# Second feed-forward projection's token operands split into high and low parts in the first projection's stage

## The chip, the cores and the metric

The kernel runs on one core of a Trainium2 chip. The time is the device time of one launch in microseconds (us), and less is better. The kernel before took 1708.27 us, the median of three runs (1705.85 to 1709.84).

## What is computed

One decoder layer for a prompt of 1024 tokens and a group of 8 x 8 sample tokens, 1088 tokens in all: a normalised, conditioned input, three mixers (attention, short convolution, pooling), an output projection, and a gated feed-forward block. The change touches only the feed-forward block:

```python
def swiglu(h, w_up, w_down):
    a, b = jnp.split(h @ w_up, 2, axis=-1)
    return (jax.nn.silu(a) * b) @ w_down
    ...
    x = x + gate1 * (jnp.concatenate([o_attn, y_conv, y_pool], axis=-1) @ w_out)
    h = rms_norm(x, norm2) * (1 + scale2) + shift2
    x = x + gate2 * swiglu(h, w_up, w_down)
```

The model width is 1024, the hidden width 2816, which is 22 tiles of 128. Everything is float32.

## The kernel before, in words

**Layout and products.** Features lie on the 128 partitions, tokens along the free dimension in four quarters of 272. Both projections use a Strassen-Winograd scheme: a 2 x 2 block product by seven products. In the first projection the two token blocks are two quarters (pair p = 0: quarters 0 and 1, p = 1: quarters 2 and 3). Each float32 operand of a product is written as a high part, rounded to the matmul's float32r format, and a low part, the rest; a product is then three matmuls (high x high, high x low, low x high). `split` (L163) makes the two parts: one ACT activation for the high part and one subtraction on DVE, or on POOL, for the low part.

**First projection** (`ffn`, L1623, and `up`, L1533). It goes over 22 hidden tiles j. For each j there is a unit for p = 0 and one for p = 1, of seven products with twelve matmuls each. DVE and ACT combine the banks to the gated hidden block `f_g`, which POOL finishes (L1581). Beside it the weights of the next j are summed (`w_s`, mostly POOL) and split (`w_hi` on ACT, `w_lo` on DVE).

**Between the two** (`down_operands`, L1586). The seven token operands that the second projection wants of a pair of hidden tiles (k = j // 2, eleven of them) and a p are three blocks as they are and four differences `f_T`, made on POOL. `store` sends each to the DRAM tensor `g_d` in float32; the list `forming` spreads the differences over the steps of the following p = 0 unit, one per product.

**Second projection** (`down_run`, L1793). It goes over six groups e of hidden tile pairs: two pairs in each of the first five groups, one in the last (`DOWN`, L30). A group is four passes (h = output half, p) of seven products and two output tiles: 28 x 2 slots, 336 matmuls in a full group, 168 in the last. `down_tokens` (L1715) loads each operand (`g_raw`) and splits it (`g_hi` on ACT, `g_lo` on DVE or POOL). `down_weights` (L1680) loads, sums (`w_s`, POOL) and splits the weights (`w_lo` or `d_lo`, DVE) of each half. After a product the bank goes to the residual x2: either straight by DVE (`down_gate`, L1745, which reads the bank) or by ACT into `d_m` (L1755) and from there by a POOL addition `x<-x,d_m`. Which weight or token step stands in which slot is a list of due slots (`down_plan`, L1760). x2 itself is loaded from `x1_d` at the start of this stage (`x1_load`, L1804).

The program is recorded in this order and then reordered per engine by a scheduler. All loads and stores named here go through SP's one queue, in its order.

Of the kernel before, what the change touches and what calls it, by code (L numbers as in the profile page):

```python
# [29 lines left out]
DOWN = (2, 2, 2, 2, 2, 1)  # L30
# [30 lines left out]
class Kernel:  # L61
# [1471 lines left out]
    def up(self, fp, j, p, W, H, step):  # L1533
# [4 lines left out]
        for y, x in enumerate(PRODUCTS):  # L1538
# [47 lines left out]
    def down_operands(self, pool, j, p, g, r):  # L1586
# [3 lines left out]
        end = j == NH - 1 and p  # L1590

        def store(dst, src):
            if end:
                nc.gpsimd.dma_start(dst, src)
            else:
                self.stores.append((self.steps + 2, dst, src))

        if j % 2:
            store(self.g_d[:, p, 1:3, j // 2], g)
        else:  # L1600
            store(self.g_d[:, p, 0, j // 2], g[:, 0])
# [5 lines left out]
        def form(x, a, b):  # L1607
            T[x] = pool.tile([P, HALF], F32, name="f_T", bufs=4)
            self.combine(T[x], a, T[b] if isinstance(b, int) else b, OP.subtract, HALF, r, "pool")
            store(self.g_d[:, p, STORED[x], j // 2], T[x])  # L1610

        self.forming += [lambda v=v: form(*v) for v in ((5, B1[:, 1], B1[:, 0]), (6, B2[:, 1], 5), (4, B2[:, 0], 6),
                                                        (7, B2[:, 1], B1[:, 1]))]
        if end:
# [8 lines left out]
    def ffn(self, wp, fp, H, state, ahead):  # L1623
# [21 lines left out]
        for n, (j, ps) in enumerate(runs):  # L1645
# [3 lines left out]
            for z, p in enumerate(ps):  # L1649
# [4 lines left out]
                def step(y, z=z, last=last, m=len(ps)):  # L1654
# [3 lines left out]
                    if self.forming and (not last or j == NH - 1):  # L1658
                        self.forming.pop(0)()
# [55 lines left out]
    def down_tokens(self, pool, steps, out):  # L1715

        nc = self.nc
        raw = []

        def load():  # L1720
            if todo:
                k0, q, e, p, x = todo.pop(0)
                t = pool.tile([P, 2, HALF], F32, name="g_raw", bufs=4)
                nc.sync.dma_start(t[:, :q], self.g_d[:, p, STORED[x], k0:k0 + q])
                raw.append((t, self.use("dma", 0.38 * q, self.t["pe"]) + 2.0))

        todo = list(steps)
        for _ in range(3):
            load()
        yield  # L1730
        for k0, q, e, p, x in steps:
            load()
            t, at = raw.pop(0)
            hi = pool.tile([P, 2, HALF], F32R, name="g_hi", bufs=15)
            lo = pool.tile([P, 2, HALF], F32R, name="g_lo", bufs=15)
            f = lambda a: a[:, :q].rearrange("p k t -> p (k t)")
            self.split(f(hi), f(lo), f(t), q * HALF, at, None)
            out[e, p, x] = (hi, lo)
# [21 lines left out]
    def down_plan(self):  # L1760

        k0, groups = 0, []
        for q in DOWN:
            groups.append((k0, q))
            k0 += q
        W, G, plan = {}, {}, []
        tok = [(k0, q, e, p, x) for e, (k0, q) in enumerate(groups) for p in range(2) for x in DOWN_PRODUCTS]
        self.d_tok = None
        for e, (k0, q) in enumerate(groups):
# [406 lines left out]
```

## Time and profile before

| | us |
|---|---|
| median of three runs | 1708.27 |
| the profiled execution | 1706.47 |
| its span, first to last instruction | 1704.6 |
| first projection's units, roughly | 930 to 1437 |
| second projection's matmuls, roughly | 1437 to 1697 |
| TensorE busy over the span | 1609.1 (94%) |
| DVE, ACT, POOL busy | 1113.6, 817.8, 706.9 |

Times within the run are microseconds from the start of the span. A busy matmul row overlaps its neighbours, so lost matmul time is read here from the number of matmuls in a stretch, not from the busy share.

### The profile page before, as it was taken

How to read it: one execution, taken by the hardware profiler on the slowest of the kernel's cores; microseconds unless marked ns; L12 is line 12 of the kernel's file. 1: busy time of each engine (PE TensorE's matmuls, PEld its weight loads, DVE VectorE, ACT ScalarE, POOL GpSimd, SP SyncE). 2: the span in 40 equal slices, each digit the busy share in tenths (PEclk: the TensorE clock that was granted, in tenths of full speed). 3: DMA queues.
4: the chain of work that ended last, by engine and by line, in shares of the span. 5: the costliest groups of instructions: out<-in, count | busy, mean ns of one | idle time of the engine just before them, and what ended most of it. 6: DMA issues, size and time to landing. Idle time of an engine off the chain costs nothing. (4 is left out here: it accounts for less than half of the span.)

```text
span 1704.6 us, 34455 instructions
## 1 busy us (share of the span) xinstructions
PE 1609.1 (94%) x11961; PEld 1414.5 (83%) x11961; DVE 1113.6 (65%) x2830; ACT 817.8 (48%) x1878; POOL 706.9 (41%) x814
## 2 busy tenths in 40 slices
PE   6999999998998999999899789999999999889998
PEld 2999997887776566666699779999999998889997
DVE  4603326686665766866699986555555556988877
ACT  3512215245766776766675643332333334555554
POOL 3101110013331322222106476445555555898976
PEclk9899999998999999999999989999999999999999
DMA  9555564226654644432783223225222225744423
GB/s 341 170 179 177 162 208 143 80 63 196 196 171 125 199 138 146 143 92 83 233 244 90 92 72 117 96 97 191 97 100 96 96 97 187 240 128 132 131 82 122
DMA packets 177120, 245.08 MB, mean 144 GB/s; under 512 B 25889, under 2 KB 132578, under 8 KB 176626
## 3 DMA queue, kind: packets, MB, share of 16 engines
q1 hardware_dynamic: 157090, 215.37, 40.4%
q0 software_dynamic: 5840, 16.10, 2.9%
q10 hardware_dynamic: 14016, 11.41, 2.2%
q8 instruction: 95, 1.56, 0.4%
q14 instruction: 79, 0.65, 0.1%
HBM read 202.33 MB, written 44.67 MB: 145 GB/s over the span
## 5 line engine op out<-in xcount | busy, mean ns | idle before, releaser
L135 PE MATMUL bank<-b_hi,w_hi 128*128 128x272 f32 x1232 | 352.3, 292 | 9.2 <-DVE f_v L1551 4.5
L135 PE MATMUL bank<-b_lo,w_hi 128*128 128x272 f32 x1232 | 356.0, 291 | 2.9 <-DVE b_lo L160 2.9
L135 PE MATMUL bank<-b_hi,w_lo 128*128 128x272 f32 x1232 | 352.0, 290 | 1.3 <-DVE w_lo L160 1.3
L135 PEld LDWEIGHTS bank<-b_hi,w_hi 128*128 128x128 f32 x1232 | 232.3, 191 | 12.3 <-ACT b_hi L164 5.1
L135 PEld LDWEIGHTS bank<-b_lo,w_hi 128*128 128x128 f32 x1232 | 234.4, 190 | 4.5 <-DVE b_lo L160 4.4
L135 PEld LDWEIGHTS bank<-b_hi,w_lo 128*128 128x128 f32 x1232 | 233.1, 190 | 2.5 <-DVE w_lo L160 2.3
L160 POOL TENSOR_TENSOR w_s<-w_raw 128x512 f32<-128x512 f32 (+1 forms) x122 | 167.3, 1373 | 149.4 <-DVE w_lo L160 133.0
L1050 POOL TENSOR_SCALAR P<-P,st 128x128 f32<-128x128 f32 (+12 forms) x192 | 112.0, 592 | 259.2 <-DVE st L1048 86.3
L160 DVE TENSOR_TENSOR w_lo<-w_raw,w_hi 128x512 fp32r<-128x512 f32 (+2 forms) x129 | 115.0, 898 | 100.7 <-ACT w_hi L164 85.8
L164 ACT ACTIVATE w_hi<-w_raw 128x512 fp32r<-128x512 f32 (+2 forms) x130 | 86.4, 674 | 150.5 <-PE bank L135 100.5
L160 DVE TENSOR_TENSOR w_lo<-w_s,w_hi 128x512 fp32r<-128x512 f32 (+1 forms) x144 | 130.3, 908 | 43.1 <-ACT w_hi L164 39.2
L160 POOL TENSOR_TENSOR x<-x,d_m 128x272 f32<-128x272 f32 x144 | 140.1, 994 | 22.9 <-DVE x L1745 11.1
L135 PE MATMUL bank<-stream 128*128 128x128 f32 x1056 | 134.1, 285 | 6.8 <-DMA stream<-in_cacheA 6.7
L135 PEld LDWEIGHTS bank<-stream 128*128 128x128 f32 x1056 | 129.0, 200 | 13.8 <-issue 8.7
L164 ACT ACTIVATE w_hi<-w_s 128x512 fp32r<-128x512 f32 (+1 forms) x144 | 89.0, 624 | 102.4 <-PE bank L135 51.5
L135 PE MATMUL bank<-h_hi,w_hi 128*128 128x384 f32 (+1 forms) x384 | 130.9, 341 | 2.4 <-ACT py L865 2.3
L135 PE MATMUL bank<-h_hi,w_lo 128*128 128x384 f32 (+1 forms) x384 | 127.1, 331 | 0.0
L1042 ACT ACTIVATE P<-P,st 128x128 f32<-128x128 f32 (+12 forms) x192 | 113.2, 591 | 28.4 <-DVE st L1033 13.8
L135 PE MATMUL bank<-h_lo,w_hi 128*128 128x384 f32 (+1 forms) x384 | 126.6, 330 | 0.0
L135 PE MATMUL bank<-g_hi,w_hi 128*128 128x272 f32 x308 | 91.8, 300 | 14.5 <-DVE x L1745 8.2
L139 PEld LDWEIGHTS bank<-ident,P 128*128 128x128 f32 (+1 forms) x592 | 63.2, 138 | 50.7 <-issue 33.6
L1033 DVE CUSTOM_DVE_ANT_0 P<-bank,m_slc 128x256 f32<-128x256 f32 (+5 forms) x136 | 68.1, 513 | 54.2 <-PE bank L135 29.2
(368 smaller groups left out, 4114.8 us busy)
## 6 DMA issues: line engine op xcount, KB each, us to landing
wada<-in_wada SPq DMA_DIRECT2D x96, 256.0 KB, 5.3
stream<-in_cacheA SPq DMA_DIRECT2D x192, 128.0 KB, 3.3
w_raw<-in_wup SPq DMA_DIRECT2D x48, 512.0 KB, 4.3
unit<-in_cacheB SPq DMA_DIRECT2D x152, 128.0 KB, 2.3
g_raw<-g_d SPq DMA_DIRECT2D x70, 272.0 KB, 3.1
stream<-in_cacheB SPq DMA_DIRECT2D x104, 128.0 KB, 2.2
w_raw<-in_wout SPq DMA_DIRECT2D x24, 512.0 KB, 4.7
g_d<-f_T SPq DMA_DIRECT2D x84, 136.0 KB, 1.8
```

The lines of the kernel that those rows point to most:

```text
L135: return self.nc.tensor.matmul(out, lhsT, rhs, start=start, stop=stop, skip_group_check=chain)
L139: self.nc.tensor.transpose(out, in_, self.ident)
L160: (self.nc.vector if eng == "dve" else self.nc.gpsimd).tensor_tensor(out, a, b, op=op)
L164: self.nc.scalar.activation(hi, src, AF.Copy)
L1033: nc.vector.tensor_tensor_reduce(out=Pt[:, h, col:col + n], in0=S[:, p0:p0 + n], in1=mk, scale=-1.0, scalar=3e38, op0=OP.add, op1=OP.min, ...
L1042: nc.scalar.activation(Ps, Ps, AF.Exp, scale=-1.0, bias=sy[:, 0:1], accum_out=sy[:, 1:2])
L1050: nc.gpsimd.tensor_scalar(Ps, Ps, sy[:, 3:4], 0.0, op0=OP.mult, op1=OP.add)
```

## The change

Lines are those of the two files; the changed file's are some 6 to 15 higher at the same place.

- The seven operands of a pair of hidden tiles and a p are split in the first projection's stage, by `split` with `eng=None`, into a new tile `f_s` (three buffers, in a pool `gs` on the left side), and stored to `g_d` as high and low part side by side. The differences are made two to a tile, so a set is stored by four DMAs in place of six. Each set has eight steps in `forming`, which now advances in every unit: seven steps in a p = 0 unit, three (products 0, 3 and 6) in a p = 1 unit.
- Three of the 22 sets stay as they were (k = 0 with p = 0, and k = 10 with both p): they go unsplit to a DRAM tensor `g_r` and are split in the second projection.
- `DOWN` becomes (1,2), (3,4), (5,6), (7,8), (9), (0,10): the group with one pair is now the fifth, and the last holds pairs 0 and 10.
- Tokens of the first five groups are loaded with both parts by one DMA straight into the operand tile `g` (14 buffers); only the last group's are split there.
- The operands of p = 0 of the first projection (`b_hi`, `b_lo`) are one tile per product and part, as large as a `g` tile, where they were one per i with all seven products in it; `g` tiles later lie where they were.
- The second pass' tokens of the first group are issued after the first x2 loads, and the second half's weights of that group are due later.

```diff
-DOWN = (2, 2, 2, 2, 2, 1)
+DOWN = ((1, 2), (3, 4), (5, 6), (7, 8), (9,), (0, 10))
+RAW = (0, 10)
...
+            if i == 0:
+                self.first = [[pool.tile([P, 4, HALF], F32R, name=f"b_{x}{y}") for x in ("hi", "lo")] for y in range(7)]
+            hi, lo = [[self.first[y][x][:, i] for y in range(7)] for x in range(2)]
...
+        def parts(src, x0):
+            src = T[src] if isinstance(src, str) else src
+            n = src.shape[1]
+            if j == NH - 1 or j == NH - 2 or j < 2 and p == 0:
+                dst = self.g_r[:, p, x0:x0 + n, RAW.index(j // 2)]
+                if j == NH - 1 and p:
+                    nc.gpsimd.dma_start(dst, src)
+                else:
+                    self.stores.append((self.steps + 1, dst, src))
+                return
+            t = self.gs.tile([P, 2, 2, HALF], F32R, name="f_s", bufs=3)
+            self.split(t[:, 0:n, 0], t[:, 0:n, 1], src, n * HALF, self.t["pe"], None)
+            self.stores.append((self.steps + 1, self.g_d[:, p, x0:x0 + n, j // 2], t[:, 0:n].bitcast(F32)))
...
-                    if self.forming and (not last or j == NH - 1):
+                    if self.forming and (not last or j == NH - 1 or y % 3 == 0):
...
+            t = pool.tile([P, 2, 2, HALF], F32R, name="g", bufs=14)
+            if e < len(DOWN) - 1:
+                self.nc.sync.dma_start(t.bitcast(F32)[:, :q], self.g_d[:, p, STORED[x], ks])
+            else:
+                src, at = raw.pop(0)
+                if p:
+                    self.nc.sync.dma_start(t.bitcast(F32)[:, 0], self.g_d[:, p, STORED[x], 0])
+                self.split(t[:, p:, 0], t[:, p:, 1], src[:, p:], (2 - p) * HALF, at, None)
+                load(1)
...
-                plan.append((at - 8, ("w", e, h)))
-                plan += [(at + 1 + 3.7 * y, ("w", e, h)) for y in range(7)]
+                plan.append((at + 6 if (e, h) == (0, 1) else at - 8, ("w", e, h)))
+                first, every = (14, 1.9) if (e, h) == (0, 1) else (1, 3.7)
+                plan += [(at + first + every * y, ("w", e, h)) for y in range(7)]
...
-            next(self.d_tok)
+            self.d_tok_n += 1
+            with self.tc.issue_after(self.x_first.ins) if 7 < self.d_tok_n <= 14 else ExitStack():
+                next(self.d_tok)
...
-                                with self.tc.issue_after(self.last_share.ins) if slot < 14 else ExitStack():
+                                with self.tc.issue_after(self.last_share.ins) if slot < 42 else ExitStack():
```

**SP's queue at the seam of the two projections.** `x_...<-x_d` are the loads of x2, by quarter: before, 17648, 17649, 17647, 17646 are quarters 0, 1, 2, 3; after, 17749, 17750, 17748, 17747. First the kernel before:

```order
L1621 DMA g_d<-f_T 128x272
L1724 DMA g_raw<-g_d 128x544 x2
L1621 DMA g_d<-f_T 128x272
L1724 DMA g_raw<-g_d 128x544 x6
L1807 DMA x_17648<-x_d 128x4x272
L1807 DMA x_17649<-x_d 128x4x272
L1807 DMA x_17647<-x_d 128x4x272
L1807 DMA x_17646<-x_d 128x4x208
L1724 DMA g_raw<-g_d 128x544
```

and the changed kernel at the same place:

```order
L1632 DMA g_r<-f_g 128x272
L1700 DMA w_raw<-in_wdown 128x2x512 x2
L1744 DMA g<-g_d 128x1088 x6
L1632 DMA g_r<-f_g 128x2x272
L1744 DMA g<-g_d 128x1088
L1632 DMA g_r<-f_T 128x2x272
L1700 DMA w_raw<-in_wdown 128x2x512 x2
L1632 DMA g_r<-f_T 128x2x272
L1821 DMA x_17749<-x_d 128x4x272
L1821 DMA x_17750<-x_d 128x4x272
L1744 DMA g<-g_d 128x1088 x7
L1821 DMA x_17748<-x_d 128x4x272
```

Two x2 loads now stand ahead of the second pass' seven token loads, and quarters 2 and 3 behind them; each token load moves twice the bytes.

**DVE in the first projection's stage**, somewhat past its middle, over the first products of one unit. Before:

```order
L1551 TENSOR_TENSOR f_m<-f_m,bank 128x272
L160 TENSOR_TENSOR w_lo<-w_s,w_hi 128x512
L160 TENSOR_TENSOR w_lo<-w_raw,w_hi 128x512
L1551 TENSOR_TENSOR f_v<-bank,f_m 128x272
L160 TENSOR_TENSOR w_lo<-w_s,w_hi 128x512
L1551 TENSOR_TENSOR f_v<-f_v,bank 128x272
```

After:

```order
L1557 TENSOR_TENSOR f_m<-f_m,bank 128x272
L161 TENSOR_TENSOR w_lo<-w_s,w_hi 128x512
L161 TENSOR_TENSOR f_s<-f_g,f_s 128x2x272
L161 TENSOR_TENSOR w_lo<-w_raw,w_hi 128x512
L1557 TENSOR_TENSOR f_v<-bank,f_m 128x272
L161 TENSOR_TENSOR f_s<-f_T,f_s 128x2x272
L161 TENSOR_TENSOR w_lo<-w_s,w_hi 128x512
L1557 TENSOR_TENSOR f_v<-f_v,bank 128x272
L161 TENSOR_TENSOR f_s<-f_T,f_s 128x2x272
```

The three double-width subtractions of a set stand between the bank readings that TensorE's next products wait for.

**DVE from the fifth into the sixth group of the second projection**, where the last group's weights and tokens are made in the changed kernel (`w_lo` and `d_lo` are the weights of its two halves, `g` its tokens):

```order
L161 TENSOR_TENSOR w_lo<-w_s,w_hi 128x512 x2
L161 TENSOR_TENSOR g<-g_raw,g 128x2x272
L1758 SCALAR_TENSOR_TENSOR x_17748<-bank,mod,x_17748 128x272
L161 TENSOR_TENSOR g<-g_raw,g 128x2x272
L161 TENSOR_TENSOR d_lo<-w_raw,d_hi 128x512
L1758 SCALAR_TENSOR_TENSOR x_17748<-bank,mod,x_17748 128x272
L1758 SCALAR_TENSOR_TENSOR x_17750<-bank,mod,x_17750 128x272
L161 TENSOR_TENSOR g<-g_raw,g 128x2x272
```

These are the only token subtractions left on DVE in the second projection: seven of double width and four of single width, with three more of single width on POOL; before there were 73 on DVE and 11 on POOL.

## Rows read from the trace of the kernel before

**Rows 1.** The page's first part: busy time, share of span, instructions of each engine.

```profile
PE 1609.1 (94%) x11961; PEld 1414.5 (83%) x11961; DVE 1113.6 (65%) x2830; ACT 817.8 (48%) x1878; POOL 706.9 (41%) x814
```

**Rows 2.** Stretches: length, busy us (instructions) of PE, PEld, DVE, ACT, POOL; clock, DMA, GB/s.

```profile
1060.00:1400.00 340.00, 338.51 (x2702) 338.08 (x2701) 190.48 (x320) 103.48 (x209) 171.19 (x161) 1.00 0.32 110
1400.00:1430.00 30.00, 30.00 (x241) 30.00 (x241) 15.79 (x27) 11.13 (x22) 12.77 (x12) 1.00 0.34 106
1430.00:1470.00 40.00, 33.20 (x224) 32.17 (x223) 33.73 (x53) 20.37 (x45) 29.62 (x29) 0.87 0.91 296
1470.00:1630.00 160.00, 149.26 (x1155) 145.56 (x1154) 144.20 (x231) 96.07 (x217) 143.00 (x121) 1.00 0.47 135
1630.00:1680.00 50.00, 48.37 (x383) 47.93 (x382) 39.50 (x83) 24.87 (x68) 36.70 (x44) 1.00 0.21 59
1680.00:1697.00 17.00, 16.40 (x121) 15.18 (x119) 13.84 (x39) 8.63 (x27) 14.28 (x20) 1.00 0.47 161
```

**Rows 3.** Waits of PE from 1380 to the end: us in all, times, longest.

```profile
PE bank L135 <- DVE x L1745: 8.7, 8, 3.0
...
PE bank L135 <- DVE g_lo L160: 2.0, 1, 2.0
PE bank L135 <- ACT g_hi L164: 1.6, 1, 1.6
```

**Rows 4.** Stretches of one us at the seam, columns as in rows 2.

```profile
1438.00:1439.00 1.00, 0.12 (x1) 0.00 (x0) 0.93 (x2) 1.00 (x3) 0.00 (x0) 1.00 0.68 257
...
1442.00:1443.00 1.00, 0.80 (x3) 0.80 (x4) 1.00 (x2) 0.50 (x1) 0.76 (x1) 0.50 0.84 170
```

**Rows 5.** SP's queue in order of time at the seam: start, us, issues.

```profile
1434.39 9.30 SPq L1724 DMA_DIRECT2D g_raw<-g_d  x6
1443.74 9.23 SPq L1807 DMA_DIRECT2D x<-x_d  x4
```

**Rows 6.** DVE in order of time: start, us, instruction, idle time before it and its end.

```profile
1427.68 0.71 DVE L160 TENSOR_TENSOR g_lo<-g_raw,g_hi 128x544 fp32r<-128x544 f32 x1
...
1451.15 0.91 DVE L1745 SCALAR_TENSOR_TENSOR x<-bank,mod,x 128x272 f32<-128x272 f32 x2 [3.45 <-DMA x<-x_d]
```

**Rows 7.** One tile's instructions, 1437 to 1705: ns min/median/max, starts, forms.

```profile
L160 DVE TENSOR_TENSOR g_lo<-g_raw,g_hi x68: 424/882/1817, 1439.0 to 1676.3; 128x544 fp32r<-128x544 f32 x57, 128x272 fp32r<-128x272 f32 x11
L160 POOL TENSOR_TENSOR w_s<-w_raw x21: 733/1670/1778, 1461.2 to 1671.3; 128x512 f32<-128x512 f32 x17, 128x256 f32<-128x256 f32 x4
L1745 DVE SCALAR_TENSOR_TENSOR x<-bank,mod,x x192: 418/487/502, 1451.2 to 1697.6; 128x272 f32<-128x272 f32 x144, 128x208 f32<-128x208 f32 x48
L160 POOL TENSOR_TENSOR x<-x,d_m x144: 752/957/1278, 1451.8 to 1696.4; 128x272 f32<-128x272 f32 x144
```

**Rows 8.** The same view in the first projection, 1040 or 1200 to 1400.

```profile
L160 DVE TENSOR_TENSOR w_lo<-w_raw,w_hi x34: 675/693/1270, 1048.3 to 1392.7; 128x512 fp32r<-128x512 f32 x34
L160 POOL TENSOR_TENSOR w_s<-w_raw x38: 1272/1288/1300, 1199.2 to 1395.3; 128x512 f32<-128x512 f32 x38
L160 POOL TENSOR_TENSOR f_T<-f_g x38: 757/776/1229, 1039.6 to 1398.2; 128x272 f32<-128x272 f32 x38
```

**Rows 9.** Instruction groups by form, 1470 to 1697: count, busy us, mean ns, idle before.

```profile
L160 POOL TENSOR_TENSOR x<-x,d_m 128x272 f32<-128x272 f32 x133 | 128.4, 987 | 15.5 <-ACT d_m L1755 6.0 <-DVE x L1745 5.5 <-ACT d_m L1757 2.5
L160 DVE TENSOR_TENSOR g_lo<-g_raw,g_hi 128x544 fp32r<-128x544 f32 x46 | 48.4, 1054 | 0.4 <-ACT g_hi L164 0.4
```

**Rows 10.** In order of time: the last of TensorE, of DVE, and SP's output stores.

```profile
1696.42 0.29 PE L135 MATMUL bank<-g_hi,d_lo 128*128 128x272 f32 x1
...
1698.56 0.48 DVE L1819 TENSOR_TENSOR x<-x,x2s 128x64 f32<-128x64 f32 x3
...
1674.63 26.80 SPq L1821 DMA_DIRECT2D out_yT<-x  x32
```

**Rows 11.** SP's queue around a large copy in the first projection.

```profile
1152.15 0.60 SPq L1675 DMA_DIRECT2D out_winKV<-in_swinKV  x1
...
1159.52 17.66 SPq L1621 DMA_DIRECT2D g_d<-f_g  x2
```

More of the change, by code (lines that the diff above doesn't have):

```diff
@@ L1589, in down_operands @@
         self.hidden[j, p] = g
[L1590 to L1601, printed above, removed]
         if (j ^ 1, p) not in self.hidden:
@@ L1607, in form @@
         def form(x, a, b):
-            T[x] = pool.tile([P, HALF], F32, name="f_T", bufs=4)
+            u, v = {5: ("A", 0), 6: ("A", 1), 7: ("C", 0), 4: ("C", 1)}[x]
+            if v == 0:
+                T[u] = pool.tile([P, 2, HALF], F32, name="f_T", bufs=2)
+            T[x] = T[u][:, v]
             self.combine(T[x], a, T[b] if isinstance(b, int) else b, OP.subtract, HALF, r, "pool")
[L1610 to L1614, printed above, removed]
+        def parts(src, x0):
[11 more added lines that the diff above has]
+            self.stores.append((self.steps + 1, self.g_d[:, p, x0:x0 + n, j // 2], t[:, 0:n].bitcast(F32)))
+        self.forming += [lambda f=f, v=v: f(*v) for f, v in (
+            (form, (5, B1[:, 1], B1[:, 0])), (form, (7, B2[:, 1], B1[:, 1])), (parts, (B1[:, 0:1], 0)),
+            (form, (6, B2[:, 1], 5)), (form, (4, B2[:, 0], 6)), (parts, (B2, 1)), (parts, ("A", 3)), (parts, ("C", 5)))]
+        if j == NH - 1 and p:
             while self.forming:
@@ L1715, in down_tokens, with load @@
     def down_tokens(self, pool, steps, out):
[L1717 to L1738, printed above, removed]
+        raw, todo = [], [v for v in steps if v[2] == len(DOWN) - 1]
+        def load(n):
+            for ks, q, e, p, x in todo[:n]:
+                t = self.dp.tile([P, 2, HALF], F32, name="g_raw", bufs=3)
+                self.nc.sync.dma_start(t[:, p:], self.g_r[:, p, STORED[x], p:])
+                raw.append((t, self.use("dma", 0.75 - 0.37 * p, self.t["pe"]) + 2.0))
+            del todo[:n]
+        for ks, q, e, p, x in steps:
+            if (e, p, x) == (len(DOWN) - 2, 1, DOWN_PRODUCTS[-1]):
+                load(3)
+            t = pool.tile([P, 2, 2, HALF], F32R, name="g", bufs=14)
+            if e < len(DOWN) - 1:
+                self.nc.sync.dma_start(t.bitcast(F32)[:, :q], self.g_d[:, p, STORED[x], ks])
+            else:
+                src, at = raw.pop(0)
+                if p:
+                    self.nc.sync.dma_start(t.bitcast(F32)[:, 0], self.g_d[:, p, STORED[x], 0])
+                self.split(t[:, p:, 0], t[:, p:, 1], src[:, p:], (2 - p) * HALF, at, None)
+                load(1)
+            out[e, p, x] = (t[:, :, 0], t[:, :, 1])
             yield
@@ L1821, in done @@
             nc.sync.dma_start(self.o["yT"][:, m, c * HALF:c * HALF + HALF], t)
-        for e, (k0, q) in enumerate(groups):
+        for e, (_, q) in enumerate(groups):
             for h in range(2):
```

41 lines of the change are left out of this document (22 added, 19 removed).

## The prediction

> **What bounds the kernel now.** I first read the page's totals: TensorE is busy for 94% of the span, DVE for 65% [rows 1], so the end can only come nearer where TensorE still waits. Then the stretches, by TensorE's count of instructions [rows 2]. From 1060 to 1400 it does 2702 in 340 us and from 1400 to 1430 241 in 30 us: 8.0 per us, or 0.125 us a matmul, is full pace. The first projection runs at that pace. From 1430 to 1470 there are 224 where 320 would fit (12.0 us lost), from 1470 to 1630 1155 of 1280 (15.6 us), from 1630 to 1680 383 of 400 (2.1 us), from 1680 to 1697 121 of 136 (1.9 us). The second projection thus loses 31 us, and its last matmul is 8 us ahead of the end of the span [rows 10].
>
> Why it loses them: PE's waits in that stage end with DVE's bank reading (8.7 us), with g_lo (2.0) and g_hi (1.6) [rows 3]. From 1470 to 1630 DVE is busy for 144.2 of 160 us and POOL for 143.0 [rows 2]. They also stretch each other. POOL's addition of x and d_m takes 0.752 us at its shortest and 1.278 at its longest; the DVE operation that reads a bank and one SBUF tile stays between 0.418 and 0.502 [rows 7]; w_lo, with two SBUF inputs, goes from 0.675 to 1.270 [rows 8]. The Trainium skill, in "SBUF — State Buffer", section "Who interferes with whom", says why: a DVE operation with two SBUF inputs and a GpSimd operation that reads SBUF exclude each other for the whole instruction. These rows agree.
>
> So I count **what the pair DVE and POOL must do one after the other**, at the shortest durations: POOL's addition 0.755 us, its weight sum 1.29 us at 512 wide [rows 8] and 0.74 at 256 [rows 7], the DVE subtraction 0.69 at 512 [rows 8], 0.71 at 544 [rows 6], 0.42 at 256 or 272 [rows 7]. A full group of the second projection has 24 additions (18.1 us), 8 sums (10.3), 14 weight subtractions (9.7) and 14 token subtractions (9.9): 48.0 us, against 336 matmuls in 42.0. The whole stage has 144 additions (108.7), some 36 wide and 8 narrow sums (52.3), 63 wide and 14 narrow weight subtractions (49.4) and 84 of tokens (55.6): 266 us, and it lasts 260, from 1437 to 1697. The pair bounds the second projection before the change.
>
> **The change, part by part.**
>
> *Second projection, groups one to four.* 56 token activations and 56 subtractions go, and a group's demand on the pair falls from 48.0 to 38.1 us, below TensorE's 42.0. The 15.6 us lost up to 1630 shrink to some 3: at 90% load in-order queues still wait now and then. Loading grows: 14 tokens of 544 KB and four weights of 512 KB in 42 us are 9.7 MB, 231 GB/s; the stage already saw 296 GB/s [rows 2]. I cost it at nothing; its cover is the lead that the due slots leave: 27 to 21 slots of 0.75 us (six matmuls) for a pass of p = 0, 20 to 13 for p = 1, so 10 to 20 us.
>
> *Groups five and six.* Here the order of groups turns against it. The fifth has 168 matmuls (21.0 us), yet the last group's wide weights and tokens are made beside it. From the fifth group's start to the middle of the sixth TensorE needs 42.0 us. The pair has 36 additions (27.2), 8 wide and 4 narrow sums (13.3), 14 wide and 7 narrow weight subtractions (12.6), 7 wide and 7 narrow tokens (7.9): 61.0 us. In full that would be 19 us lost. Six d_m buffers let six additions run late (4.5 us), the last weights are due one product after another (some 4), and each earlier group leaves 3.9 us of which the scheduler can use one or so: I take 7 us, between 2 and 19. Before, these two groups lost 4.0 (2.1 and 1.9). So over the groups 15.6 + 4.0 become 3 + 7: 9.6 us saved.
>
> *The seam.* Before, TensorE waits 1.6 us for g_hi and 2.0 for g_lo [rows 3], and does one matmul from 1438 to 1439; after that idle time the granted clock stands at 0.50, the lower of its two levels (1.2 of 2.4 GHz) [rows 4]. Then the first bank waits for x2, which lands at 1451 [rows 6]: its loads stand in SP's queue behind six g_raw, which take 9.3 us to issue because each waits for a buffer that ACT and DVE must free, and start at 1443.7 [rows 5]. Now the first pass' tokens come ready split, into memory that products 0 to 3 of the unit before leave, and two x2 loads stand ahead of the second pass' tokens. But those seven tokens (3.8 MB) stand ahead of quarters 2 and 3: at 296 GB/s [rows 2] two x2 loads and seven tokens take 17 us, two more x2 loads 4, so from 1438 quarters 2 and 3 land near 1460, and the second pass wants a bank back that only they free 24 slots of 0.75 us after 1437, at 1455. I let 5 of the 12.0 us stay lost (between 1 and 12): 7 saved.
>
> *First projection.* 19 sets are added, each with three wide subtractions and one narrow, 2.55 us, 48 us in all. ACT takes its share easily (103.5 of 340 us busy [rows 2]). The pair's demand for one j, two units of 10.5 us, is now seven w_lo (4.8), five sums of which one is DVE's (5.9) and six POOL operations at 0.76 [rows 8] (4.6): 15.3 of 21.0 us. It becomes 17.9, 85%. It is uneven: the p = 1 unit, with five of seven weights, goes from 8.5 to 10.4 of 10.5 us, since three steps of a set now fall there. A late bank reading costs TensorE at once, for the next product but one adds to the same bank. The bound from below is nothing, as the row of 1060 to 1400 shows no loss at 56% DVE; from above I take 15 us, the same as the groups before lost at 48 to 42. Near the lower one, as the average stays under TensorE's time: 4 us. A gain lies beside it: the store queue stood for 17.7 us behind the large copy [rows 11]; with four stores in place of six per set fewer weight loads are caught behind it: 1 us. Net 3 lost.
>
> *The end.* The last group is now a full one, its additions fewer per matmul; the 8 us after the last matmul, with output stores still leaving one per 0.84 us (32 in 26.8 [rows 10]), become some 5.5: 2.5 saved.
>
> **Sum**: 9.6 + 7 + 2.5 - 3 = 16 us as it stands. The two large terms lean on the scheduler meeting its due slots, so of the 9.6 I keep 7, as a new wait in the second half of the fifth group would reach TensorE through full banks: 13.5. The profiled execution took 1706.47, so 1693.0; it stands 1.8 below the median, so 1695 for the median.
>
> **The rivals.**
>
> *The last two groups cost nothing and the seam closes.* The scheduler has room in the fourth group, and the additions can lag. Then the groups lose 3 in place of 10, the seam 2 in place of 5, and the 2.5 kept back come too: 12 us more, about 1683. For it: in the old last group, also 21.0 us long, the pair had 24 additions, and TensorE still lost only 1.9 us [rows 2]. Against it: 61.0 us of work in 42.0.
>
> *The last two groups lose all of it.* By the rule of "SBUF — State Buffer" in the Trainium skill the pair never overlaps, and the stretch loses all of its 19 us. By rows: POOL's addition averages 0.987 us and the wide g_lo 1.054 [rows 9], so the excess does reach the queues. That is 12 us more than my 7, near 1707: no measurable change.
>
> *The first projection pays more than the second saves.* The split now sits between the readings of banks that TensorE waits for. If the p = 1 units overrun and the loss passes into TensorE, the price is a wait per unit. The other terms save 16.5 net of what is kept back, over 38 units 0.43 us each: from there on it is slower. With a wide subtraction stretched to 1.05 us [rows 9] ahead of a bank reading in two thirds of the units, 38 x 0.68 = 26 us are lost: 1718 or so, taken as 1717. Against it: the average demand of 85%, and half-idle p = 0 units beside.
>
> That the change doesn't do what it says is no rival: the order shows the subtractions in their new place, and the loads at the seam in theirs.
>
> **How the numbers follow.** Forecast 0.58, at 1695, its own range 1688 to 1702. The better rival 0.17, the even one 0.13, the slower one 0.12. Measurement can tell 0.2%, 3.4 us, from no change: faster is below 1704.9, slower above 1711.7. Faster: 0.58 + 0.17 + 0.05 of the even case = 0.80. Same: the rest of it, 0.08, and 0.02 of the slower case = 0.10. Slower 0.10. Range 1682 to 1708: it takes in the better and the even case and leaves out the slower one and the ends of the others, two in ten.
>
> **What would show it.** Right: from the first group's end to the fourth's full pace, DVE near 70% busy there; POOL's addition nearer 0.85 than 0.987 us; clock 1.00 at the seam up to about 1455; the loss gathered around the fifth group. Wrong: fewer than 2660 matmuls in 340 us of the first projection (5 us); PE waits that end with DVE's f_v; x2 quarters 2 and 3 landing after 1465; PE idle for g.

## The result, and the profile after

The changed kernel takes 1697.13 us, the median of four runs (1696.78 to 1697.30), against 1707.69 of the kernel before on the same chip (1705.85 to 1709.84): a ratio of 0.9941, 95% interval 0.9928 to 0.9954. The forecast was 1695. The profiled execution took 1697.3 us with a span of 1695.7, 8.9 less than before.

The page's first part, answering [rows 1]:

```profile
PE 1605.4 (95%) x11961; PEld 1409.9 (83%) x11961; DVE 1122.6 (66%) x2852; ACT 819.0 (48%) x1884; POOL 680.1 (40%) x797
```

The stretches of the changed kernel, columns as in [rows 2]:

```profile
1060.00:1400.00 340.00, 336.60 (x2668) 334.43 (x2669) 251.00 (x390) 134.48 (x272) 171.65 (x152) 1.00 0.44 154
1400.00:1430.00 30.00, 30.00 (x240) 29.83 (x240) 18.20 (x35) 10.76 (x23) 13.56 (x13) 1.00 0.47 172
1430.00:1470.00 40.00, 34.27 (x251) 34.05 (x250) 15.92 (x30) 13.61 (x31) 22.43 (x25) 0.91 0.88 317
1470.00:1630.00 160.00, 158.58 (x1258) 157.77 (x1257) 113.01 (x227) 74.07 (x186) 126.78 (x133) 1.00 0.69 241
1630.00:1680.00 50.00, 45.04 (x342) 43.26 (x341) 40.70 (x82) 26.52 (x67) 44.11 (x43) 1.00 0.46 144
1680.00:1697.00 17.00, 10.92 (x88) 10.70 (x86) 6.64 (x23) 2.68 (x9) 4.58 (x6) 0.91 0.33 112
...
1452.00:1456.00 4.00, 3.76 (x16) 3.76 (x17) 1.43 (x4) 1.69 (x5) 3.62 (x6) 0.50 1.04 413
```

At 8.0 matmuls per us the time moved like this. From 1020 to 1430 there are 55 matmuls fewer (20 of them before 1060): 6.9 us lost. From 1430 to 1470, 27 more: 3.4 saved. From 1470 to 1630 the loss falls from 15.6 to 2.75 us, while that of the last two groups, from 1630 on, rises from 4.0 to 7.25: 9.6 saved. The end after the last matmul shrinks from 7.9 to 4.8 us. Sum: 9.6 + 3.4 + 3.1 - 6.9 = 9.2, against the measured 8.9.

PE's waits from 1380 on, answering [rows 3]; the waits for `g_lo` and `g_hi` are gone:

```profile
PE bank L136 <- ACT d_m L1768: 7.3, 3, 5.7
PE bank L136 <- DVE x L1758: 3.8, 5, 1.7
PE bank L136 <- POOL g L161: 0.8, 1, 0.8
PE bank L136 <- ACT d_m L1770: 0.3, 1, 0.3
```

The longest one, 5.7 us, is the seam. In order of time there (SP's queue, then DVE, ACT with its queue, POOL, PE; columns as in [rows 5, 6]):

```profile
1437.24 1.08 SPq L1700 DMA_DIRECT2D w_raw<-in_wdown  x2
...
1441.27 1.77 SPq L1821 DMA_DIRECT2D x<-x_d  x2
1443.91 19.72 SPq L1744 DMA_DIRECT2D g<-g_d  x7
1463.80 5.13 SPq L1821 DMA_DIRECT2D x<-x_d  x6
...
1451.31 0.48 DVE L1876 MEMSET x<- 128x512 f32 x1 [8.47 <-DMA x<-x_d]
1451.71 0.81 DVE L1758 SCALAR_TENSOR_TENSOR x<-bank,mod,x 128x272 f32<-128x272 f32 x2
...
1451.10 0.55 ACTq L1843 DMA_DIRECT2D x2s<-x_d  x1
1451.70 0.86 ACT L1768 ACTIVATE d_m<-bank,mod 128x272 f32<-128x272 f32 x2 [9.19 <-POOL f_T L161]
...
1448.38 1.27 POOL L161 TENSOR_TENSOR w_s<-w_s,w_raw 128x512 f32<-128x512 f32 x1
1449.60 0.76 POOL L161 TENSOR_TENSOR f_T<-f_g 128x272 f32<-128x272 f32 x1
1450.31 0.76 POOL L161 TENSOR_TENSOR f_T<-f_g,f_T 128x272 f32<-128x272 f32 x1
...
1452.24 0.82 PE L136 MATMUL bank<-g,w_hi 128*128 128x272 f32 x2 [5.73 <-ACT d_m L1768]
```

The last matmul of the first projection starts at 1442.07 (1435.24 before), PE goes on with `g` at once, and stops at 1446.5. Two things end within half a microsecond. ACT's queue stands behind its load of `x2s` until POOL's last `f_T` ends at 1451.07, and the bank copies `d_m` stand behind that load; on DVE the clearing of `x2`'s last columns stands in front of the gates. And the first two `x2` loads, though issued 2.5 us sooner than before, are still landing: the first gate starts at 1451.71, before at 1451.15 [rows 6]. The rings carry 408 GB/s from 1450 to 1460. After the wait the clock is 0.50 for some four microseconds: 16 matmuls where 32 would fit.

Groups one to four come out as forecast: DVE is busy 113.0 of 160 us (144.2 before), and POOL's addition is shorter (0.900 us on average, 0.987 before). The loads, costed at nothing, cost nothing there: 241 GB/s, and no wait of PE's that ends with a load. By form from 1470 to 1697, answering [rows 9]:

```profile
L161 POOL TENSOR_TENSOR x<-x,d_m 128x272 f32<-128x272 f32 x138 | 121.2, 900 | 35.3 <-DVE x L1758 22.9 <-ACT d_m L1768 8.1 <-ACT d_m L1770 3.2
L161 DVE TENSOR_TENSOR g<-g_raw,g 128x544 fp32r<-128x544 f32 x7 | 8.4, 1206 | 0.0
```

The end, in order of time, answering [rows 10]:

```profile
1690.64 0.29 PE L136 MATMUL bank<-g,d_lo 128*128 128x272 f32 x1
...
1691.71 0.21 DVE L1834 TENSOR_TENSOR x<-x,x2s 128x64 f32<-128x64 f32 x1
...
1663.34 29.96 SPq L1836 DMA_DIRECT2D out_yT<-x  x30
```

### The profile page after: what moved, and what is told of

Its sections match the earlier page's. It is cut to its first block, busy times and chain, and to the rows that moved or that the text cites. A ratio compares the mean times of both kernels' runs of the same rounds, so it can differ in the third digit from the quotient of the medians.

```text
span 1695.7 us, 34350 instructions
## 1 busy us (share of the span) xinstructions
PE 1605.4 (95%) x11961; PEld 1409.9 (83%) x11961; DVE 1122.6 (66%) x2852; ACT 819.0 (48%) x1884; POOL 680.1 (40%) x797
## 4 chain that ended last, share of the span: by engine, by line
PE 70%; DVE 12%; DMA 6%; ACT 4%; issue 3%; POOL 2%; SPq 1%; ACTq 0%; POOLq 0%; DVEq 0%
PE bank L136 65%; PE bank L140 5%; DVE w_lo L161 3%; DVE b_lo L161 1%; DMA wada<-in_wada 1%; DMA stream<-in_cacheA 1%; SPq L518 1%; DVE x L1758 1%; DMA w_raw<-in_wup 1%; POOL w_s L161 1%; DVE n_ss L161 1%; ACT w_hi L165 1%; DMA stream<-in_wtok 1%; DMA w_raw<-in_wout 1%; ACT stream L151 1%
## 5 line engine op out<-in xcount | busy, mean ns | idle before, releaser
L161 DVE TENSOR_TENSOR w_lo<-w_raw,w_hi 128x512 fp32r<-128x512 f32 (+2 forms) x129 | 125.2, 978 | 94.7 <-ACT w_hi L165 94.1
L161 POOL TENSOR_TENSOR w_s<-w_raw 128x512 f32<-128x512 f32 (+1 forms) x106 | 149.6, 1412 | 71.2 <-DVE w_lo L161 53.5
L161 DVE TENSOR_TENSOR w_lo<-w_s,w_hi 128x512 fp32r<-128x512 f32 (+1 forms) x144 | 134.7, 940 | 19.5 <-ACT w_hi L165 15.1
L161 POOL TENSOR_TENSOR x<-x,d_m 128x272 f32<-128x272 f32 x144 | 125.6, 894 | 35.7 <-DVE x L1758 22.9
L136 PE MATMUL bank<-g,w_hi 128*128 128x272 f32 x616 | 122.3, 294 | 8.4 <-ACT d_m L1768 6.7
L1043 ACT ACTIVATE P<-P,st 128x128 f32<-128x128 f32 (+12 forms) x192 | 113.2, 591 | 30.3 <-DVE st L1034 15.6
L136 PE MATMUL bank<-g,d_hi 128*128 128x272 f32 x616 | 118.7, 290 | 3.7 <-DVE x L1758 3.1
L1758 DVE SCALAR_TENSOR_TENSOR x<-bank,mod,x 128x272 f32<-128x272 f32 (+1 forms) x192 | 87.2, 476 | 42.2 <-PE bank L136 34.5
```

The source lines that it names most:

```text
L136: return self.nc.tensor.matmul(out, lhsT, rhs, start=start, stop=stop, skip_group_check=chain)
L161: (self.nc.vector if eng == "dve" else self.nc.gpsimd).tensor_tensor(out, a, b, op=op)
L1043: nc.scalar.activation(Ps, Ps, AF.Exp, scale=-1.0, bias=sy[:, 0:1], accum_out=sy[:, 1:2])
L1758: nc.vector.scalar_tensor_tensor(out[:, :n], acc[:, :n], self.mod[:, 5, m, 0:1], out[:, :n], op0=OP.mult, op1=OP.add)
```

## The experiments

All are edits of the changed kernel. Their times are medians, each with its ratio to runs of the kernel before on the same chip; those runs spread over up to 12 us, so a ratio is good to some 0.15%, and most verdicts rest on counts of matmuls. The last four columns are these counts, from one profiled execution of each kernel, which lies up to 3.6 us from the kernel's median (9: 1696.61 us); the first of the four is the sum of 1020 to 1060 and 1060 to 1400.

| kernel | us | ratio (95%) | 1020-1400 | 1430-1470 | 1470-1630 | 1630-1680 |
|---|---|---|---|---|---|---|
| before | 1707.69 | 1 | 3012 | 224 | 1155 | 383 |
| the change | 1697.13 | 0.9941 (0.9928-0.9954) | 2958 | 251 | 1258 | 342 |
| 1 queues freed | 1696.12 | 0.9945 (0.9933-0.9958) | 2956 | 248 | 1256 | 340 |
| 2 fewer tokens | 1701.44 | 0.9981 (0.9968-0.9993) | 2961 | 249 | 1247 | 343 |
| 3 both | 1693.77 | 0.9928 (0.9912-0.9944) | 2962 | 307 | 1218 | 360 |
| 4 weights after x2 | 1700.17 | 0.9963 (0.9949-0.9976) | 2954 | 258 | 1230 | 344 |
| 5 old layout | 1698.53 | 0.9954 (0.9939-0.9970) | 2963 | 252 | 1257 | 344 |
| 6 groups swapped | 1691.85 | 0.9923 (0.9907-0.9939) | 2961 | 257 | 1257 | 393 |
| 7 steps in p = 0 only | 1698.79 | 0.9956 (0.9939-0.9973) | 2959 | 258 | 1253 | 343 |
| 8 no low parts | 1690.69 | 0.9902 (0.9884-0.9920) | 3017 | 251 | 1235 | 358 |
| 9 differences first | 1700.23 | 0.9968 (0.9954-0.9982) | 2957 | 249 | 1253 | 343 |
| 10 low parts on POOL | 1706.47 | 1.0002 (0.9986-1.0018) | 2895 | 252 | 1266 | 333 |
| 11 6 and 1 | 1693.62 | 0.9925 (0.9900-0.9950) | 2965 | 251 | 1250 | 393 |
| 12 11, first pass unhalved | 1686.00 | 0.9881 (0.9858-0.9905) | 2979 | 290 | 1251 | 377 |

Kernels alike up to 1400 (the change, 1 to 4, 6 and 11) count 2954 to 2965 there, and those alike at the seam (the change, 6 to 10) 249 to 258 from 1430 to 1470: differences of that size (about 1.4 us) say nothing. The last two columns don't show a loss in one place: in 3 and 8 the fifth group comes sooner and part of its loss falls before 1630, and in 12 the last matmul starts at 1678.83.

### The seam: 1, 2, 3

Experiment 1 keeps the load of `x2s` and the clearing where the program has them.

```diff
-  nc.scalar.dma_start(xs, self.x1_d[:, :, SEQ:])
+  with self.tc.issue_after(self.last_share.ins):
+      nc.scalar.dma_start(xs, self.x1_d[:, :, SEQ:])
...
-  if slot == 9:
-      nc.vector.memset(x2[3][:, :, n3:], 0.0)
+  if slot == 17:
+      with self.tc.issue_after(self.last_gate.ins):
+          nc.vector.memset(x2[3][:, :, n3:], 0.0)
```

> Edit: at the seam the load of x2s keeps its place (second group) on ScalarE's queue, and the clearing of the last token columns of x2 its place (slot 17) on VectorE's queue; neither stands in front of the first readings of the banks any more. Theory Q (the two queues were blocked: x2s load and clearing waited for the memory that POOL's last f_T, ended at 1451.07, gave free, and bank readings stood behind them): PE's wait of 5.7 us on the d_m copy goes, PE counts 278 to 290 matmuls in 1430 to 1470 instead of 251, time 1692.5 to 1694. Rival D (the DMA queues bound the seam: the first two x2 loads, issued at 1441.27 behind seven tokens of 544 KB, land only at about 1451, so that VectorE's gates could not have begun sooner): PE gets through 12 more matmuls (1.5 us) at once, then waits for a gate that waits for x<-x_d until about 1451; count 255 to 265, time 1695.5 to 1697.

Experiment 2 leaves three tokens out (in `down_tokens`).

```diff
+  if e == 0 and p == 0 and x in (7, 3, 4):
+      out[e, p, x] = out[0, 0, {7: 1, 3: 2, 4: 6}[x]]
+      yield
+      continue
```

> Left out: the tokens of products 7, 3 and 4 of the first group's first half of the columns are not loaded; those of products 1, 2 and 6 are used in their place, so 1.6 MB (about 4 us at the 390 to 408 GB/s seen there) less stands in front of the x2 loads. Theory Q (queues blocked by POOL's f_T chain until 1451): POOL's chain doesn't change, the stall until 1452 stays, time within 1 us of the change's 1697.1. Rival D (DMA bounds the seam and the wait named POOL was really one for x2): the x2 loads land at about 1447, the stall ends about 4 us sooner, time about 1693.

Experiment 3 has both edits.

> The two edits together: x2s load and clearing keep their places, and the tokens of products 7, 3 and 4 of the first group's first half are left out (those of products 1, 2 and 6 stand in). If the queues alone were the cause (Q), this gives what the first edit gives, 1692.5 to 1694. If both bind at the same moment (f_T's end and x2's landing both at 1451), each edit alone gives 0 to 1.5 us and the two together 4 to 6 us: 1691 to 1693, PE count in 1430 to 1470 about 290.

PE's waits from 1438 to 1470 and the landing of the first two `x2` loads (min, median, max from issue) in experiment 1:

```profile
PE bank L136 <- DVE x L1758: 6.4, 1, 6.4
...
DMA to landing us min/median/max: 10.4/11.1/11.7
```

in experiment 3:

```profile
PE bank L136 <- DMA g<-g_d: 0.5, 1, 0.5
PE bank L136 <- DVE x L1762: 0.2, 1, 0.2
...
DMA to landing us min/median/max: 4.9/5.4/5.9
```

and the landing of the same loads in the change:

```profile
DMA to landing us min/median/max: 10.2/10.2/10.2
```

With the queues free, PE does 14 matmuls more before 1450 (66 against 52) and then waits 6.4 us for a gate that waits for `x2` (rival D, though the count, 248, is below its 255 to 265). With the bytes alone taken away `x2` lands after 5.5 to 6.5 us, at 1448, but PE waits 7.1 us for `d_m`, as the queues are still blocked (theory Q). What frees them there isn't POOL's last `f_T`, which ends at 1449.42: ACT and DVE are released by the store `g_r<-f_g`, at about 1452.8. With both edits the stall is gone and the clock stays at 1.00. Two causes bound the seam and ended together; each edit alone gains nothing. At the seam that is 56 matmuls, 7.0 us, more than the 4 to 6 forecast; the time fell by 3.4 only, to 1693.77, just above the 1691 to 1693 forecast. Some 3 us came back from 1470 to 1550 (606 matmuls, 631 in the change), where PE waits 1.6 us for a gate of DVE's and 1.5 for a `d_m`. Experiment 2 was to be within 1 us of the change by theory Q, 4 us faster by rival D, and is 4 us slower; its profiled execution (1699.3 us) shows 1.4 of that as the longer wait, and the rest stays open.

### The seam: 4, 5

Experiment 4 is 1, with the loads of the first group's second weights behind the first `x2` loads.

```diff
-  next(self.d_w[e, h])
+  with self.tc.issue_after(self.x_first.ins) if (e, h) == (0, 1) else ExitStack():
+      next(self.d_w[e, h])
```

> Edits: x2s load and clearing keep their places as in the first run, and the loads of the first group's second weights (1 MB, issued at 1437.24) are queued behind the first two x2 loads, which also puts POOL's two w_s sums behind the last f_T. From the first four runs: queues and x2's landing bind at the same moment. The theory that both bind (QD): x2 lands 2.7 us (1 MB at 390 GB/s) sooner, PE's wait on the gate of 6.4 us falls to 3 to 4, count in 1430 to 1470 goes from 252 to 275 to 290, time 1692.5 to 1694.5. Rival (the seven tokens of the second pass, queued behind x2, share the rings with it and take what is freed): wait 5 to 6.5 us, count below 265, time as the first run's 1696.

`x2` landed after 6.1 to 8.9 us and the wait fell to 3.2, but a new one of 2.1 us came at 1469 for the gates of quarters 2 and 3, and DVE's gates cost PE 8.7 us in all from 1438 on. The wait is the theory's 3 to 4 us, the count, 258, the rival's, and the time, 1700.17, longer than either's. Putting 1 MB later gains nothing here: what it gives at the first gates it takes back at the next ones.

Experiment 5 undoes the layout of the first quarters' operands alone.

```diff
-  if p:
+  if True:
       hi, lo = [pool.tile([P, 7, HALF], F32R, name=f"b_{x}{i}") for x in ("hi", "lo")]
```

> Edit: the second part of the change alone is undone: the operands of the first quarters are laid out by row block as before, not by product, so that the first tokens of the second projection can be written only when the last unit on these quarters has ended (about 1431), not product by product from 1418. Theory QD (the rings are full at the seam and x2 waits behind the tokens): 3.3 MB move from 1418 to 1434 into 1431 to 1441, at 390 GB/s 8 us of transfer of which half finds the rings idle; x2's landing moves from 1451 to about 1455, PE's wait of 5.7 us becomes 8 to 11, and PE may wait for g itself; count in 1430 to 1470 falls from 251 to 215 to 235, time 1699.5 to 1702. Rival N (the tokens are early anyway and x2 waits for the memory of the first projection): time within 1 us of the change, count 245 to 255.

The first six tokens are now issued from 1432.05 in place of 1417.96, the first `x2` loads at 1443.02 in place of 1441.27; the wait is 6.9 us against 5.7. That is nearest the rival (count 252; 1.4 us slower where it allowed 1): the layout by product is worth about a microsecond of wait, below what the times resolve. The rings had room until 1440 (busy share 0.73 from 1430, 1.05 from 1440 on, in the change), so the stall seems to be set by what comes after.

### The last two groups: 6

```diff
-DOWN = ((1, 2), (3, 4), (5, 6), (7, 8), (9,), (0, 10))
+DOWN = ((1, 2), (3, 4), (5, 6), (7, 8), (0, 10), (9,))
```

(`down_tokens` halves the fifth group's operands in place of the last one's.)

> Edit: the last two groups change places: pairs (0, 10), whose operands are halved on ScalarE and VectorE in this stage, become the fifth group, and the group of one pair, (9), becomes the last. Theory G (VectorE and POOL, which hold each other up, have 10 of 10 us each in 1630 to 1650, because the halving for the last group falls beside the half-size fifth group): the halving now falls beside the fourth group, which has twice the matmuls, and beside nothing at the end; the 7.25 us lost in 1630 to 1680 shrink to 2 to 4, and a loss of 1 to 3 us comes back in 1560 to 1630, where POOL and VectorE have about 8 of 10. The end gets a little longer, since the last group's stores have half the time (10.5 us for 4.4 MB) : 0 to 4 us. Time 1692 to 1697. Rival T (the loss there is the order of the weights of a small group, w_raw and w_s of q=1, and not the load of the pair): the loss moves with the small group to the end, 7 us stay, time 1697 to 1701.

One stretch, columns as in [rows 2], of the change and then of experiment 6:

```profile
1630.00:1650.00 20.00, 16.72 (x121) 15.35 (x119) 20.00 (x33) 14.22 (x36) 20.00 (x17) 1.00 0.53 164
```

```profile
1630.00:1650.00 20.00, 20.00 (x162) 20.00 (x161) 9.99 (x25) 7.34 (x21) 12.01 (x16) 1.00 0.29 85
```

DVE and POOL were both busy for the whole 20 us; now they are half free, and PE is at full pace. Theory G holds, and better than forecast: from 1470 to 1630 nothing came back (1257), and the end grew from 4.8 to 5.5 us only. The change's own order of groups cost it 5 to 6 us by the counts (51 matmuls, less the longer end) and by the medians (5.3); by the ratios it is 3, with intervals that overlap.

### The first projection: 7 to 10

Experiment 7 advances a set's steps in p = 0 units only.

```diff
-  if self.forming and (not last or j == NH - 1 or y % 3 == 0):
-      self.forming.pop(0)()
+  for _ in range(1 + (len(self.forming) > 6)) if not last or j == NH - 1 else ():
+      if self.forming:
+          self.forming.pop(0)()
```

> Edit: a set's steps advance only in p=0 units as before the change, two at a time while more than six wait, and no longer in p=1 units, which make five of the seven weights. The change lost 6.9 us more than the kernel before in 1020 to 1400 (290 and 2668 matmuls in 1020:1060 and 1060:1400, against 310 and 2702). Theory L (the load: in p=1 units DVE and POOL have 10.4 of 10.5 us, and bank readings come late): with that load in p=0 units the loss shrinks to 3 us or less, counts near 305 and 2690, time 1693 to 1695. Rival A (ScalarE's queue in order: high-part copies f_s stand in front of bank readings while they wait for POOL's f_T and f_g): two steps at a time bunch copies and what they wait for, the loss stays or grows, counts at most 290 and 2668, time 1697 to 1700.

Experiment 8 leaves out the low parts (in `parts`; `t` is one of three fixed buffers).

```diff
-  self.split(t[:, 0:n, 0], t[:, 0:n, 1], src, n * HALF, self.t["pe"], None)
+  nc.scalar.activation(t[:, 0:n, 0], src, AF.Copy)
```

> Left out: the low parts of the operands that the first projection halves (the subtraction on VectorE, or POOL, after each high-part copy); three fixed buffers, whose low halves hold zeros, stand in for the rotating ones. The high-part copies on ScalarE, their order, and all stores stay. Theory L (load of the pair VectorE and POOL, 2.55 us a set): the loss in 1020 to 1400 goes back to that of the kernel before, counts 305 to 312 and 2695 to 2705, some 5 to 7 us saved, time about 1691. Rival A (copies in front of bank readings on ScalarE, waiting for POOL): the waits on f_m and f_g stay at 3.5 us or more in all, counts at most 295 and 2680, time 1695 to 1697.

Experiment 9 puts a set's four differences ahead of its halvings.

```diff
-  (form, (7, ...)), (parts, (B1[:, 0:1], 0)), (form, (6, ...)), (form, (4, ...)), (parts, (B2, 1)),
+  (form, (7, ...)), (form, (6, ...)), (form, (4, ...)), (parts, (B1[:, 0:1], 0)), (parts, (B2, 1)),
```

> Edit: a set's four subtractions on POOL come first and its three wide and one narrow halvings after them, so that a high-part copy is issued three or four steps after the f_T that it reads; nothing is added or left out. Theory A (copies waiting on POOL at the head of ScalarE's queue): PE's waits on ACT f_m and f_g in 960 to 1438 fall from 4.1 us to 2 or less, counts 300 and 2685, 3 to 4 us saved. Rival L (load alone): waits and counts stay within 1 us of the change's 290 and 2668.

Experiment 10 subtracts all low parts on POOL.

```diff
-  self.split(t[:, 0:n, 0], t[:, 0:n, 1], src, n * HALF, self.t["pe"], None)
+  self.split(t[:, 0:n, 0], t[:, 0:n, 1], src, n * HALF, self.t["pe"], "pool")
```

> Edit: the low parts of the operands that the first projection halves are all subtracted on POOL instead of mostly on VectorE. Nothing is left out. The run without these subtractions gave counts 305 and 2712 in 1020:1060 and 1060:1400 (the change 290 and 2668), so they cost the 7 us; open is how. Theory V (they stand in front of bank readings in VectorE's in-order queue): off VectorE the loss goes, counts 302 or more and 2695 or more, time 1690 to 1693. Rival X (VectorE and POOL hold each other up, so only the sum of the two counts, and POOL needs about 1.3 us for what VectorE does in 0.7): VectorE's own operations with two inputs in SBUF are stretched by POOL, counts at most 290 and 2668, time 1697 to 1702.

Without the low parts the count is 3017, as in the kernel before (3012): the subtractions cost the whole 7 us, and the high-part copies, which stay on ACT, nothing that the counts resolve. The order of the steps (9, as its rival L said) and the units that they fall in (7, as its rival A said) change nothing that the counts resolve either. In 9 PE's waits from 960 to 1438 that end with ACT's `f_m` and `f_g` fall from 4.6 to 3.3 us, but those that end with DVE's `f_v` rise from 4.6 to 6.0. So it isn't ACT's queue alone, and not the p = 1 units in particular.

Of the 55 matmuls lost, 41 are missing in two stretches: from 1050 to 1070 the change has 134 (162 before, 134 in experiment 7, 154 in 8), from 1180 to 1200 140 (153 before, 146 in 7, 163 in 8). In the first of them, of the change (POOL, DVE, ACT, PE):

```profile
1052.15 1.74 POOL L161 TENSOR_TENSOR w_s<-w_raw 128x512 f32<-128x512 f32 x1
1053.86 1.22 POOL L161 TENSOR_TENSOR f_T<-f_g,f_T 128x272 f32<-128x272 f32 x1
1055.04 1.76 POOL L161 TENSOR_TENSOR w_s<-w_raw 128x512 f32<-128x512 f32 x1
1056.77 1.22 POOL L161 TENSOR_TENSOR f_T<-f_g 128x272 f32<-128x272 f32 x1
...
1053.02 1.43 DVE L161 TENSOR_TENSOR w_lo<-w_s,w_hi 128x512 fp32r<-128x512 f32 x1
1054.37 1.29 DVE L161 TENSOR_TENSOR f_s<-f_T,f_s 128x544 fp32r<-128x544 f32 x1
1055.58 1.77 DVE L161 TENSOR_TENSOR w_lo<-w_s,w_hi 128x512 fp32r<-128x512 f32 x1
1057.28 1.30 DVE L161 TENSOR_TENSOR f_s<-f_T,f_s 128x544 fp32r<-128x544 f32 x1
...
1059.45 0.43 DVE L1557 TENSOR_TENSOR f_g<-bank,f_m 128x272 f32<-128x272 f32 x1
...
1060.25 0.38 ACT L1560 ACTIVATE f_m<-bank 128x272 f32<-128x272 f32 x1
...
1060.68 0.39 PE L136 MATMUL bank<-b_hi,w_hi 128*128 128x272 f32 x1 [1.37 <-ACT f_m L1560]
```

From 1053.9 to 1058.6 the ends of the two engines' operations alternate, and each comes 0.55 to 0.64 us (1.14 for the sum `w_s`) after the other engine's: about the operation's own shortest time (0.67 to 0.76, and 1.27 [rows 8]), less 0.1. The two engines work one after the other here. Meanwhile DVE reads no bank, and ACT's `f_m`, behind an operation that waits for DVE's `f_g`, comes 1.37 us late for PE.

On POOL the low parts cost 8 us more, against theory V. Rows from 1060 to 1400, columns as in [rows 7], of the change:

```profile
L161 DVE TENSOR_TENSOR w_lo<-w_s,w_hi x80: 674/694/1783, 1061.2 to 1398.3; 128x512 fp32r<-128x512 f32 x80
...
L1557 DVE TENSOR_TENSOR f_v<-f_v,bank x32: 423/426/439, 1064.8 to 1397.1; 128x272 f32<-128x272 f32 x32
...
L161 DVE TENSOR_TENSOR f_s<-f_T,f_s x32: 710/836/1448, 1066.4 to 1397.4; 128x544 fp32r<-128x544 f32 x32
```

and of experiment 10:

```profile
L161 DVE TENSOR_TENSOR w_lo<-w_s,w_hi x78: 677/968/1953, 1061.4 to 1399.8; 128x512 fp32r<-128x512 f32 x78
...
L1557 DVE TENSOR_TENSOR f_v<-f_v,bank x31: 423/436/440, 1064.9 to 1392.6; 128x272 f32<-128x272 f32 x31
...
L161 POOL TENSOR_TENSOR f_s<-f_T,f_s x32: 1332/1586/1885, 1058.5 to 1375.7; 128x544 fp32r<-128x544 f32 x32
```

With DVE relieved of the subtraction, its weight subtraction `w_lo` stretches from 0.694 to 0.968 us (median), while the bank reading, with one input in SBUF, stays at 0.43: the two engines hold each other up, and POOL takes 1.33 us at its shortest for what DVE does in 0.71. The Trainium skill's rule in "SBUF — State Buffer", section "Who interferes with whom", that a DVE operation with two SBUF inputs contends with a GpSimd operation that reads SBUF, agrees with these rows. This is rival X in kind, but with more lost than its 1697 to 1702: POOL's queue is now late as well, and ACT's `w_hi` waits 28.5 us in all for POOL's `w_s` from 1020 to 1400 (4.4 in the change). How much of the 8 us is stretching and how much POOL's slower pace, this run doesn't part.

### Together: 11, 12

Experiment 11 has the edits of 6 and 1.

> The two edits that moved waits and leave nothing out, together: the last two groups change places, and x2s load and clearing keep their places at the seam. If both add up: 6 to 7 us from the groups and 0 to 1 us from the seam (VectorE's gate still waits for x2), time 1690 to 1692, count in 1630:1680 395 or more of 400. If the new order of the queues costs elsewhere: 1692 to 1695.

Count 393 from the swap, nothing from the seam, whose longest wait is 6.5 us for a gate; 1693.62 lies in the second range, but its interval overlaps that of experiment 6.

Experiment 12 adds what the first ones ask for: the first group's first pass is stored unhalved and halved as it comes.

```diff
+  if p == 0 and j // 2 in DOWN[0]:
+      self.stores.append((self.steps + 1, self.g_q[:, x0:x0 + n, j // 2 - 1], src))
+      return
...
+  self.nc.sync.dma_start(t.bitcast(F32)[:, :, 1], self.g_q[:, STORED[x]])
...
+  self.split(t[:, :, 0], t[:, :, 1], t.bitcast(F32)[:, :, 1], 2 * HALF, at, "dve")
```

> Edits: the last two groups change places and x2s load and clearing keep their places (as in the run before); and the operands of the first group's first pass (pairs 1 and 2, first quarters) are stored unhalved and halved on ScalarE and VectorE as they come, as before the change. That takes 1.9 MB out of the rings just ahead of the x2 loads, where leaving out 1.6 MB closed the seam (315 matmuls in 40 us from 1430), and takes two of the 19 added sets out of the first projection. Theory (rings bound the seam, VectorE and POOL the first projection): x2 lands in 5 to 7 us instead of 10 to 11, the gates' wait of 6.5 us falls to 0.5 to 3, count in 1430:1470 from 251 to 285 to 310; first projection 0 to 1.5 us less lost; of the seam's gain up to 3 us come back as waits for x2's second half; time 1686 to 1690. Rival (seven more halvings beside the last unit hold up its bank readings on the in-order queues of ScalarE and VectorE, or the halved tokens come late): 2 to 5 us lost ahead of 1442 or a wait for g at the seam, time 1691 to 1695.

Its seam (stretch; PE's waits from 1438 to 1470; landing of the first two `x2` loads):

```profile
1430.00:1470.00 40.00, 36.99 (x290) 36.28 (x289) 29.04 (x50) 18.96 (x41) 31.30 (x33) 1.00 1.00 349
...
PE bank L137 <- DVE f_g L1558: 1.5, 1, 1.5
PE bank L137 <- DVE x L1779: 1.5, 2, 1.3
...
DMA to landing us min/median/max: 4.3/5.1/5.8
```

1686.00 us, 0.9881 of the kernel before (0.9858 to 0.9905), better than it and than the change. The rival's price is there but small: 1.5 us behind `f_g`, which stands behind two halvings on DVE. The count up to 1400, 2979, is 14 to 25 above the kernels with all 19 sets: two sets fewer give back 2 to 3 us, more than their share of 7, so it matters where they lay: 11 matmuls of it come from 1050 to 1070 (145, in the change 134). Which of the two was dear wasn't tried.

## Why the prediction was right or wrong

The direction and the mechanism held, and the time lies in the forecast's own range. Two terms were mis-sized by 3.6 and 3.9 us, and that the time still came within 2.1 us of the 1695 is in part luck: 2.6 us kept back for a wait of the groups that didn't come paid for part of them. Term by term:

| term | forecast | measured |
|---|---|---|
| groups one to four | 15.6 to 3 | 15.6 to 2.75 |
| groups five and six | 4.0 to 7 | 4.0 to 7.25 |
| kept back of these | 2.6 | 0 |
| seam | 12.0 to 5: 7 | 12.0 to 8.6: 3.4 |
| end | 2.5 | 3.1 |
| first projection | -3 | -6.9 |
| sum | 13.5 | 9.2 |

- **Groups: right.** Counting what DVE and POOL must do one after the other gave both sizes. The even rival, that the last two groups lose all 19 us, fell: 7.25. The rest of the 19 was absorbed somewhere; no run took that apart. Experiment 6 shows that the excess was one of order: the same work beside a full group costs nothing. Two slips of the working, 0.755 us for a shortest addition that the row has at 0.752, and 0.68 for two thirds of 1.05 us, change no term.
- **Seam: mis-sized, by the step "I let 5 of the 12.0 us stay lost".** I put the shortage at quarters 2 and 3 and the second pass. It came earlier. I let the first two `x2` loads land sooner because they were issued sooner; they landed after 10 us, because operands with both parts are twice the bytes just there, where the rings already ran at 390 to 408 GB/s (experiments 1 to 3, 12). And I had not looked at what the order puts in front of the first bank readings on ACT and DVE. The mark "clock 1.00 up to about 1455" was wrong for the same reason; "quarters 2 and 3 after 1465" came true too, their loads being issued from 1463.80.
- **First projection: mis-sized, by the step "Near the lower one, as the average stays under TensorE's time: 4 us".** The net loss was 6.9, not 3. The mechanism is the pair's load, but not as I placed it, in the p = 1 units: experiment 7 empties them of the new work and nothing is won. The loss lies in bursts, where a set's subtractions and the weights' meet: 41 of the 55 matmuls are missing from 1050 to 1070 and, behind the large copy, from 1180 to 1200, while 1200 to 1400 has 1594 of 1600. There the two engines work one after the other (the rows beside experiments 7 to 10), and an average over 21 us doesn't see it. The 1 us set down as a gain of the store queue behind the large copy doesn't show: from 1160 to 1200 there are ten matmuls fewer than before. The sign of being wrong, fewer than 2660 matmuls from 1060 to 1400, stayed out (2668), since 20 of the 55 lay before 1060. The rival that pays 0.43 us a unit was right in kind; the price is 0.18.
- **End: right**, 3.1 for 2.5.

The errors of -3.6 and -3.9 against +2.6 and +0.6 make the 4.3 us by which the sum was too large.

## What to carry to other kernels

Work that is moved into a stage with room was paid for here in that stage's fullest ten microseconds, so sum the demand of engines that hold each other up there, and not over the stage. An operand stored in two parts is twice the bytes: do it where the rings have room, and keep it whole where they are full and the engines that would part it stand idle. A wait's named releaser can hide a second cause that ends at the same moment; if taking the named one away gives nothing, take both away before dropping either.

## What had not been expected of the hardware

- The same two loads of 544 KB, issued at nearly the same place, took 10.2 us to land in the change, 5.4 with 1.6 MB less ahead of them and free queues, 5.1 with 1.9 MB less.
- After the wait of 5.7 us the granted clock stood at 0.50 (1.2 of 2.4 GHz) from 1452 to 1456; in experiments 3 and 12, with no wait above 1.5 us there, it stayed at 1.00 from 1430 to 1470. The stall thus cost some 2 us beyond its own length.
- ACT was held for 9.19 us by a load on its own queue that waited for memory, with `d_m` copies behind it.
